# Two data routes in a two-layer trunk: how a gate row is stored and fetched, and how a normalised stream is turned

## The chip, the cores and the metric

The kernel runs on one core of a Trainium2 chip. The metric is the device time of one execution in microseconds (us): the median of several runs. A core has a matrix engine (PE, which multiplies a loaded 128x128 "stationary" tile by a moving one; the load is listed apart as PEld), a vector engine (DVE), a scalar engine (ACT), GpSimd (POOL) and a sync engine (SP). SP, ACT and POOL also issue DMA transfers, which 16 DMA engines carry out; their issues are listed under SPq, ACTq and POOLq.

## The reference

Two token streams pass through the same two layers: P, a prompt of 128 tokens, and S, a sample of 256 tokens with a cached context. Each has its own conditioning vector. Cut to what matters here:

```python
mod = silu(cvec) @ ada_w[l] + ada_b[l]             # one row of 6*1024 per stream
sh1, sc1, g1, sh2, sc2, g2 = split(mod, 6)
h = rms_norm(x, norm1_g) * (1.0 + sc1) + sh1
mix = token_mixers(h, ...)                         # gating MLP, differential attention, GQA, then w_out
x = x + g1 * mix
h = rms_norm(x, norm2_g) * (1.0 + sc2) + sh2
x = x + g2 * peer_ffn(h, ...)                      # 8 heads, top 16 of 16384 experts each
```

with `rms_norm(x, g) = x * rsqrt(mean(x*x) + 1e-6) * g` and `D = 1024`. After layer 1 a last `rms_norm` gives the output. All is float32.

## The kernel before

A layer has two stages. `chain` runs adaLN, first norm, mixers, output projection, second norm and the product-key queries for both streams; `experts` then evaluates the experts. For S it goes densely over all 16384 of them in 128 chunks (a table chunk is loaded, split into a high and a low part by ACT and DVE, and multiplied on PE). For P it gathers the chosen rows through GpSimd (`ugt`, `vgt`) and combines them on DVE. These gathers start while S is still in `chain`. In the profiled run the four stages lie at 0 to some 486 us, to 1236, to some 1622 and to 2387.

A tile framework orders the instructions: the code yields pieces of work as tasks with costs, and a scheduler with a simulated timeline sets each engine's queue and inserts the semaphores. All engine calls go through a helper at line 82, so nearly all rows show L82; work is told apart by its tiles.

The change touches four functions:

- `ada_chunk` multiplies the conditioning vectors by one of twelve 512-column chunks of `ada_w` (tile `pada`), adds the bias `ab`, and has in `row` 128 partitions: four quarters of 128 columns, 32 partitions apart, with the streams P and S in the first two partitions of each quarter. Shift and scale chunks are turned into columns (`modT`). The four gate chunks of a layer (`which` 2 and 5) are stored whole, 128x128 numbers, to a DRAM tile `grow`.
- `gate_half` fetches half a gate row (512 numbers) from `grow` to all 128 partitions: a partition's 2 KB come as four pieces of 512 bytes. `wout` uses it (tile `wo`) to scale the output projection, and `finish`, in chunk 110 of `experts`, to load the gate `G` for the update of the residual behind the experts. Both issue from ACT's queue.
- `normed_T(st, n, ...)` is the first norm (n = 0) or the second (n = 1) of a stream, block by block (128 tokens). It must give the normed, scaled and shifted stream with features on partitions. It takes the sum of squares (ACT, `junk`), the root (`rstd_of`: DVE and one POOL power; with `newton`, for S's second norm, a chain of DVE instructions on tiles `rsqi` and `rsqt`), makes a 128x128 diagonal of the roots, `dr` (ACT), and multiplies each of the block's eight 128x128 pieces by it on PE into `pt`, which scales and transposes at once. DVE and ACT then take turns to apply `modT` into `hTs` or `hTp`.
- `gate_rows` is not called.

P's first norm of layer 1 is not among these: `next_norm`, at the end of `experts`, does it with a DVE scaling in place of `x2p` and transposes by `ident`. So `normed_T` does eleven blocks: P, S, S at the first norm of layer 0, S, S at that of layer 1 (tile `x2s`, which GpSimd also stores to DRAM), and three at each second norm. `x` in layer 0's first norm is a copy that `wout` later loads again. The buffer tagged `mixT` holds the mixers' outputs up to the output projection and the queries `qT` after the second norm. For S, `hh` and `hl` are the high and low part of the second norm's result, and `pq` are the query products.

Of the kernel before, what the change touches and what calls it, by code (L numbers as in the profile page):

```python
# [9 lines left out]
F32 = mybir.dt.float32  # L10
# [5 lines left out]
AF = mybir.ActivationFunctionType  # L16
ALU = mybir.AluOpType
AX = mybir.AxisListType

D = 1024  # L20
# [78 lines left out]
def trunk_kernel(ctx, tc, xin, silu_c, wts, adab, ccol, crow, finalg, rope, ohc, io2, skt,  # L99
                 sgut, lkT, lv, ut, ug, vg, y, ck_d, cv_d, ck_g, cv_g):  # L100
    nc = tc.nc
    V, A, TE, SY, GP = nc.vector, nc.scalar, nc.tensor, nc.sync, nc.gpsimd
# [6 lines left out]
    dpool = ctx.enter_context(tc.tile_pool(name="dpool", bufs=2, space=bass.MemoryType.DRAM))  # L109

    V, TE, A, GP = Follow(V), Follow(TE), Follow(A), Follow(GP)
# [3 lines left out]
    def bank(name, st=None):  # L115
        if st is not None and name + st.name in cur["tags"]:
            name += st.name
        tag, n = cur["tags"][name]
        return cur["psum"].tile([128, 512], F32, tag=tag, name=name, bufs=n)
# [8 lines left out]
    ident = cp.tile([128, 128], F32, name="ident")  # L128
# [18 lines left out]
    def rstd_of(ss, n, width, newton=False):  # L147
        r = sm.tile([128, 8], F32, name="rstd")
        r = r[:, 0:width]
        V.tensor_scalar(r, ss, 1.0 / n, EPS, op0=ALU.mult, op1=ALU.add)  # L150
        if newton:

            i, t = sm.tile([128, 8], U32, name="rsqi")[:, 0:width], sm.tile([128, 8], F32, name="rsqt")[:, 0:width]
            V.tensor_tensor(i, r.bitcast(U32), c1[:, 0:width], op=ALU.logical_shift_right)
            V.tensor_scalar(i, i, -1.0, float(0x5f3759df), op0=ALU.mult, op1=ALU.add)
            yv = i.bitcast(F32)
            for _ in range(3):
                V.tensor_tensor(t, yv, yv, op=ALU.mult)
                V.scalar_tensor_tensor(t, t, -0.5, r, op0=ALU.mult, op1=ALU.mult)
                V.scalar_tensor_tensor(yv, t, 1.5, yv, op0=ALU.add, op1=ALU.mult)  # L160
            return yv
        GP.tensor_tensor(r, r, mhalf[:, 0:width], op=ALU.pow)
        return r

    def transposes(cols, st=None):
        pt = bank("pt", st)
        for i, c in enumerate(cols):
            TE.transpose(pt[:, i * 128:(i + 1) * 128], c, ident)
        return pt
# [4 lines left out]
    def new_layer(l):  # L174
        L = Layer()
        L.l, L.have = l, set()
        L.lam_init = 0.8 - 0.6 * math.exp(-0.3 * l)
        L.modT = sp.tile([128, 4, KC, 2], F32, name="modT")
        L.cc = sp.tile([128, 20], F32, name="cc")
        A.dma_start(L.cc, ccol[l])  # L180
        L.grow = dpool.tile([2, 2, 128, 128], F32, name="grow")
        return L

    def ada_chunk(L, j, pieces):
        which, half = divmod(j, 2)
        L.have.add(j)
        ab = sm.tile([128, 128], F32, name="ab", bufs=2)
        A.dma_start(ab, adab[L.l, j])
        ps = bank("pada")
        k = 0  # L190
        for w in pieces:
            for kk in range(w.shape[1]):
                for q in range(4):
                    TE.matmul(ps[32 * q:32 * q + 32, 0:128], sT[:, k, :], w[:, kk, q * 128:(q + 1) * 128],
                              start=(k == 0), stop=(k == KC - 1), tile_position=(0, 32 * q))
                k += 1
        row = sm.tile([128, 128], F32, name="row", bufs=2)
        V.tensor_tensor(row, ps[:, 0:128], ab, op=ALU.add)
        if which in (2, 5):
            SY.dma_start(L.grow[which // 3, half], row)  # L200
            return
        pt = transposes([row])
        pv = pt[:, 0:128].rearrange("p (q r) -> p q r", r=32)[:, :, 0:2]
        m = {0: 0, 1: 1, 3: 2, 4: 3}[which]
        dst = L.modT[:, m, half * 4:(half + 1) * 4, :]
        if m % 2:
            g = L.cc[:, (m // 2) * 8 + half * 4:(m // 2) * 8 + half * 4 + 4]
            V.scalar_tensor_tensor(dst, pv, 1.0, g[:, :, None].to_broadcast([128, 4, 2]), op0=ALU.add, op1=ALU.mult)
        else:
            V.tensor_copy(dst, pv)  # L210

    def gate_half(L, which, half, row, gb):
        src = L.grow[which, half].rearrange("(q r) c -> q r c", r=32)[:, row, :]
        A.dma_start(gb.rearrange("p (q c) -> p q c", q=4), src[None].to_broadcast([128, 4, 128]))

    def gate_rows(L, which, row, gb):
        src = L.grow[which].rearrange("h (q r) c -> h q r c", r=32)[:, :, row, :]
        A.dma_start(gb.rearrange("p (h q c) -> p h q c", h=2, q=4), src[None].to_broadcast([128, 2, 4, 128]))


    class Retrieval:
# [64 lines left out]
    def chain(L, early_ada, Ln, R0):  # L286
        l = L.l
        with ExitStack() as es:
            tp = es.enter_context(tc.tile_pool(name=f"tp{l}", bufs=1, reuse_waits=RW))
# [9 lines left out]
            def s512(st, name, w=512):  # L299
                t = tp.tile([128, 512], F32, tag="s512" + st.name, name=name, bufs=S5[0] if st is P else S5[1])  # L300
                return t[:, 0:w]
# [73 lines left out]
            def need(*js):  # L375
                while not L.have.issuperset(js):
                    yield 1.0

            def normed_T(st, n, hT, blocks):
                yield from need(*range(6 * n, 6 * n + 4))  # L380
                for b in blocks:
                    xn = st.xs[b]
                    ss = sm.tile([128, 1], F32, name="ss")
                    A.activation(s512(st, "junk").bitcast(BF16), xn, AF.Square, accum_out=ss)
                    r = rstd_of(ss, D, 1, newton=NEWT[0] and st.past and n == 1 or NEWT[2])

                    dr = s512(st, "dr", 128)
                    A.activation(dr, ident, AF.Copy, scale=r)
                    for g in range(2):
                        pt = bank("pt", st)  # L390
                        for q in range(4):
                            k = g * 4 + q
                            TE.matmul(pt[:, q * 128:(q + 1) * 128], xn[:, k * 128:(k + 1) * 128], dr, start=True, stop=True)
                        for q in range(4):
                            k = g * 4 + q
                            o = hT[:, k, b * 128:(b + 1) * 128]
                            i = pt[:, q * 128:(q + 1) * 128]
                            sca = L.modT[:, 2 * n + 1, k, st.row:st.row + 1]
                            shi = L.modT[:, 2 * n, k, st.row:st.row + 1]
                            if q % 2:  # L400
                                A.activation(o, i, AF.Identity, bias=shi, scale=sca)
                            else:
                                V.tensor_scalar(o, i, sca, shi, op0=ALU.mult, op1=ALU.add)
                    yield CN
# [427 lines left out]
            def head(st):  # L832
                if not st.past and R0 is not None and LEFT:
                    while R0.n < NSLOT + R0.LAG:
                        yield 1.0
                    for half in range(2):
                        hs = slice(half * 512, (half + 1) * 512)
                        gb = s512(st, "gb")
                        gate_half(R0.L, 1, half, st.row, gb)
                        V.tensor_tensor(gb, R0.acc[:, hs], gb, op=ALU.mult)  # L840
                        V.tensor_tensor(st.xs[0][:, hs], st.xs[0][:, hs], gb, op=ALU.add)
                    xd = dpool.tile([128, D], F32, name="x2p")
                    SY.dma_start(xd, st.xs[0])
                    st.x[0] = xd
                elif st.next:
                    st.xs, st.next = st.next, {}
                else:
                    st.xs = {}
                    for b in range(st.nb):
                        load_x(st, b)  # L850
                if not st.past:
                    alloc_mix(st)
                    if st.hT is not None:
                        return
                hp = pp if st.past else tp
                st.hT = hp.tile([128, KC, st.T], F32, name=f"hT{st.name}")
                yield from normed_T(st, 0, st.hT, range(st.nb))
# [139 lines left out]
    def experts(L, R, Ln):  # L997
        l = L.l
        last = l == DEPTH - 1
        with ExitStack() as es:  # L1000
# [246 lines left out]
            dense_loop()  # L1247

    L, R = new_layer(0), None
    for l in range(DEPTH):  # L1250
        Ln = new_layer(l + 1) if l + 1 < DEPTH else None
        R = chain(L, l == 0, Ln, R)
        R.L = L
        experts(L, R, Ln)
        L = Ln
# [86 lines left out]
```

## Time and profile before

| | us |
|---|---|
| median of three runs | 2394.32 |
| lowest, highest | 2392.46, 2396.28 |
| profiled execution, own time | 2388.71 |
| its span, first to last instruction | 2386.9 |
| mean granted PE clock | 0.968 of full |

The profiled execution is 5.6 us (0.23%) under the median; 1.8 us of its time lie outside its span. In the profile a row "out<-in" names the tile written and the tiles read, "xN" is the count, and "[2.19 <-ACT dr]" says that the engine had been idle for 2.19 us until ACT's work on `dr` released it. PEclk is the share of full clock that was granted to PE.

### The profile page before, as it was taken

The numbers are of one execution on the slowest core, as the hardware profiler recorded it, in microseconds if no ns is written. First come the engines' busy times: TensorE is split into PE (matmuls) and PEld (weight loads), VectorE is DVE, ScalarE is ACT, GpSimd is POOL, SyncE is SP. The second block draws the span as 40 slices with busy tenths as digits, with TensorE's granted clock in tenths as the row PEclk, the third lists the DMA queues.
The fourth block names the chain that finished last, engine by engine and source line by source line (L and its number), as shares of the span: only waits on it lengthen the run. The fifth ranks groups of instructions, "written<-read, shape, count | busy, mean of one in ns | idle before, by whom it ended". The sixth has DMA issues, their size and how long they took to land.

```text
span 2386.9 us, 38803 instructions
## 1 busy us (share of the span) xinstructions
PE 2218.8 (93%) x14466; PEld 1726.2 (72%) x14466; DVE 1860.0 (78%) x3795; ACT 894.4 (37%) x1848; POOL 755.0 (32%) x558
## 2 busy tenths in 40 slices
PE   6999879889999989999999998797999999999997
PEld 4446537676898768899974464586689877889996
DVE  1234668987999959899962466899889996999996
ACT  2224311143444334444442343114344343444443
POOL 0000043103544425455400002400345443545540
PEclk9998989999999999999999999899999999999999
DMA  8665699738998869999976424942899887999994
GB/s 331 211 221 175 215 356 360 275 111 293 369 376 319 287 224 400 366 375 383 367 257 203 130 89 147 356 138 90 291 356 388 336 285 260 394 386 383 380 374 161
DMA packets 201998, 681.25 MB, mean 285 GB/s; under 512 B 22225, under 2 KB 37201, under 8 KB 201809
## 3 DMA queue, kind: packets, MB, share of 16 engines
q1 hardware_dynamic: 112448, 397.66, 45.8%
q0 software_dynamic: 74160, 270.04, 30.7%
q10 hardware_dynamic: 15200, 11.07, 1.9%
q8 instruction: 114, 1.87, 0.3%
q14 instruction: 76, 0.61, 0.1%
HBM read 671.08 MB, written 7.60 MB: 284 GB/s over the span
## 4 chain that ended last, share of the span: by engine, by line
PE 71%; DVE 15%; DMA 9%; ACT 2%; issue 2%; ACTq 0%; POOL 0%; DVEq 0%; SPq 0%; POOLq 0%
PE acc L82 27%; PE pP L82 23%; PE mm L82 10%; DMA raw<-in_vg 3%; DMA w<-in_wts 3%; PE pt L82 3%; PE sc L82 2%; PE pG L82 2%; DVE ugt L82 2%; DVE si L82 2%; DVE pacc L82 2%; DVE lo L82 2%; DMA ugt<-in_ug,ei 1%; PE pq L82 1%; PE pg L82 1%
## 5 line engine op out<-in xcount | busy, mean ns | idle before, releaser
L82 POOL DMA_INDIRECT ugt<-in_ug,ei x256 | 360.8, 1409 | 975.9 <-DVE ugt L82 811.7
L82 DVE TENSOR_TENSOR lo<-raw,hi 128x1024 fp32r<-128x1024 f32 x418 | 504.9, 1220 | 108.5 <-ACT hi L82 90.4
L82 ACT ACTIVATE hi<-raw 128x1024 fp32r<-128x1024 f32 x418 | 435.6, 1057 | 343.4 <-DMA raw<-in_vg 179.4
L82 PE MATMUL acc<-hi,whl 128*128 128x512 f32 x1680 | 479.5, 400 | 19.3 <-ACT whl L82 11.2
L82 PE MATMUL pP<-hh,lo 128*128 128x256 f32 x1664 | 465.9, 280 | 8.8 <-DVE lo L82 8.7
L82 PE MATMUL pP<-hh,hi 128*128 128x256 f32 x1664 | 469.1, 282 | 1.5 <-ACT hi L82 1.5
L82 PE MATMUL pP<-hl,hi 128*128 128x256 f32 x1664 | 463.1, 278 | 0.0
L82 POOL DMA_INDIRECT vgt<-in_vg,ei x256 | 362.5, 1416 | 167.7 <-DVE pacc L82 73.2
L82 PEld LDWEIGHTS acc<-hi,whl 128*128 128x128 f32 x1680 | 313.2, 191 | 88.4 <-ACT whl L82 11.8
L82 DVE SCALAR_TENSOR_TENSOR ugt<-ugt,h 128x1024 f32<-128x1024 f32 x256 | 311.7, 1218 | 28.6 <-DMA ugt<-in_ug,ei 26.9
L82 DVE SCALAR_TENSOR_TENSOR pacc<-vgt,gz,pacc 128x1024 f32<-128x1024 f32 x254 | 324.9, 1279 | 3.9 <-DMA vgt<-in_vg,ei 3.5
L82 PEld LDWEIGHTS pP<-hh,lo 128*128 128x128 f32 x1664 | 312.6, 188 | 19.4 <-DVE lo L82 12.1
L82 PEld LDWEIGHTS pP<-hh,hi 128*128 128x128 f32 x1664 | 314.4, 189 | 10.3 <-issue 3.3
L82 PEld LDWEIGHTS pP<-hl,hi 128*128 128x128 f32 x1664 | 312.7, 188 | 3.0 <-issue 0.5
L82 PE MATMUL acc<-lo,whl 128*128 128x512 f32 x840 | 264.4, 398 | 0.1
L82 PEld LDWEIGHTS acc<-lo,whl 128*128 128x128 f32 x840 | 155.8, 191 | 31.5 <-DVE lo L82 0.7
L82 ACT ACTIVATE W<-pP 128x512 f32<-128x512 f32 x104 | 62.1, 597 | 300.0 <-PE pP L82 249.6
L82 POOL TENSOR_TENSOR rstd<-rstd,mhalf 128x1 f32<-128x1 f32 (+3 forms) x34 | 29.1, 861 | 434.1 <-DVE rstd L82 434.1
L82 ACT ACTIVATE G<-pG 128x128 f32<-128x128 f32 x512 | 94.4, 301 | 76.5 <-PE pG L82 75.5
L82 PE MATMUL mm<-w,hTs 128*128 128x512 f32 x256 | 117.6, 610 | 1.9 <-DMA w<-in_wts 1.8
L82 DVE TENSOR_TENSOR o<-ohio,i12d 128x2048 f16<-128x2048 f16 (+1 forms) x128 | 117.9, 952 | 0.8 <-DMA ohio<-in_io 0.7
L82 PE MATMUL mm<-hTs,w 128*128 128x256 f32 x512 | 117.9, 387 | 0.0
(248 smaller groups left out, 2716.2 us busy)
## 6 DMA issues: line engine op xcount, KB each, us to landing
raw<-in_vg SPq DMA_DIRECT2D x256, 512.0 KB
w<-in_wts SPq DMA_DIRECT2D x224, 512.0 KB
raw<-in_ut SPq DMA_DIRECT2D x224, 512.0 KB
w<-in_ut SPq DMA_DIRECT2D x32, 512.0 KB
ugt<-in_ug,ei POOLq DMA_INDIRECT x256
vgt<-in_vg,ei POOLq DMA_INDIRECT x256
x<-in_xin SPq DMA_DIRECT2D x5, 512.0 KB
wo<-grow ACTq DMA_DIRECT2D x8, 256.0 KB
```

Of the source, the lines that this page charges most:

```text
L82: self.last = f(*a, **k)
```

## The change

There are three edits. A layer's `grow` now holds, for each of the two gates and each stream, one unbroken row of 1024 numbers, and each gate chunk is stored by two DMAs of 4x128 numbers, one for each stream, where it was one DMA of 128x128. `gate_half` reads 512 numbers in one piece for each partition. In `normed_T` the diagonal is gone: at the first norm DVE scales the block in place; at the second ACT writes a scaled copy `xm` into the `mixT` buffer; then PE transposes by `ident`.

```diff
-        L.grow = dpool.tile([2, 2, 128, 128], F32, name="grow")
+        L.grow = dpool.tile([2, 2, D], F32, name="grow")
...
         if which in (2, 5):
-            SY.dma_start(L.grow[which // 3, half], row)
+            for r in range(2):
+                SY.dma_start(L.grow[which // 3, r, half * 512:half * 512 + 512].rearrange("(q c) -> q c", q=4),
+                             row.rearrange("(q r) c -> q r c", r=32)[:, r, :])
             return
...
     def gate_half(L, which, half, row, gb):
-        src = L.grow[which, half].rearrange("(q r) c -> q r c", r=32)[:, row, :]
-        A.dma_start(gb.rearrange("p (q c) -> p q c", q=4), src[None].to_broadcast([128, 4, 128]))
-
-    def gate_rows(L, which, row, gb):
...
+        src = L.grow[which, row:row + 1, half * 512:half * 512 + 512]
+        A.dma_start(gb, src.to_broadcast([128, 512]))
...
-                    dr = s512(st, "dr", 128)
-                    A.activation(dr, ident, AF.Copy, scale=r)
+                    if n == 0:
+                        V.tensor_scalar(xn, xn, r, None, op0=ALU.mult)
+                    else:
+
+                        if b == 0:
+                            xm = tp.tile([128, st.nb, D], F32, name="xm", tag="mixT" + st.name)
+                        A.activation(xm[:, b], xn, AF.Copy, scale=r)
+                        xn = xm[:, b]
                     for g in range(2):
                         pt = bank("pt", st)
                         for q in range(4):
                             k = g * 4 + q
-                            TE.matmul(pt[:, q * 128:(q + 1) * 128], xn[:, k * 128:(k + 1) * 128], dr, start=True, stop=True)
+                            TE.transpose(pt[:, q * 128:(q + 1) * 128], xn[:, k * 128:(k + 1) * 128], ident)
```

Since the scheduler sets the queues, the instructions also stand differently. On ACT, at S's second norm in layer 1 (`gz` are P's expert gates, unrelated to the norm), the order before is:

```order
L82 DMA wo<-grow 128x4x128
L82 ACTIVATE gz<-gz 128x4
L82 ACTIVATE junk,ss<-x 128x1024
L82 ACTIVATE gz<-gz 128x4
L82 ACTIVATE dr<-ident,rsqi 128x128
L82 ACTIVATE junk,ss<-x 128x1024
L82 ACTIVATE hTs<-pt,modT 128x128 x4
L82 ACTIVATE dr<-ident,rsqi 128x128
L82 ACTIVATE hh<-hTs 128x8x128
L82 ACTIVATE hTs<-pt,modT 128x128 x4
```

The same place on ACT after:

```order
L82 DMA wo<-grow 128x512
L82 ACTIVATE gz<-gz 128x4
L82 ACTIVATE junk,ss<-x 128x1024 x2
L82 ACTIVATE xm<-x,rsqi 128x1024 x2
L82 ACTIVATE hTs<-pt,modT 128x128 x3
L82 ACTIVATE gz<-gz 128x4
L82 ACTIVATE hTs<-pt,modT 128x128
L82 ACTIVATE hh<-hTs 128x8x128
L82 ACTIVATE hTs<-pt,modT 128x128 x4
```

Both blocks' sums of squares and both scalings now stand ahead of the first `hTs`; before, the second block's diagonal stood behind the first block's.

On PE, at S's second norm in layer 0 (`mm` is the output projection), the order before is:

```order
L82 MATMUL mm<-w,mixTs 128x512 x8
L82 MATMUL pada<-w,sT 32x128 x29
L82 MATMUL pt<-dr,x 128x128 x15
L82 MATMUL pada<-w,sT 32x128 x4
L82 MATMUL pt<-dr,x 128x128
L82 MATMUL pada<-w,sT 32x128 x6
L82 MATMUL pq<-hTs,w 128x256 x8
```

The same place on PE after:

```order
L82 MATMUL mm<-w,mixTs 128x512
L82 MATMUL pada<-w,sT 32x128 x22
L82 MATMUL pt<-ident,xm 128x128 x8
L82 MATMUL pada<-w,sT 32x128 x8
L82 MATMUL pt<-ident,xm 128x128 x8
L82 MATMUL pq<-hTs,w 128x256 x4
```

Of adaLN's products, eight now stand between the two blocks' transposes and none between these and the first `pq`.

On DVE, at S's first norm in layer 1, where the instructions ahead are those that end the update of `x2s` and prepare the attention's constants, the order after is:

```order
L82 TENSOR_SCALAR nlam<-nlam 128x1
L82 TENSOR_SCALAR rstd<-ss 128x1
L82 TENSOR_SCALAR x2s<-x2s,rstd 128x1024
L82 TENSOR_SCALAR hTs<-pt,modT 128x128 x4
L82 TENSOR_SCALAR rstd<-ss 128x1
```

Before, the same rows stood there without the scaling of `x2s`, which is new work on DVE's queue between the root and the four `hTs`.

More of the change, by code (lines that the diff above doesn't have):

```diff
@@ L212, in gate_half @@
     def gate_half(L, which, half, row, gb):
-        src = L.grow[which, half].rearrange("(q r) c -> q r c", r=32)[:, row, :]
-        A.dma_start(gb.rearrange("p (q c) -> p q c", q=4), src[None].to_broadcast([128, 4, 128]))
-    def gate_rows(L, which, row, gb):
-        src = L.grow[which].rearrange("h (q r) c -> h q r c", r=32)[:, :, row, :]
-        A.dma_start(gb.rearrange("p (h q c) -> p h q c", h=2, q=4), src[None].to_broadcast([128, 2, 4, 128]))
+        src = L.grow[which, row:row + 1, half * 512:half * 512 + 512]
+        A.dma_start(gb, src.to_broadcast([128, 512]))
     class Retrieval:
```

## The prediction, made before the changed kernel ran

> **What bounds the kernel now.** I read the page first: its engines and the chain that ended last.
>
> ```profile
> span 2386.9 us, 38803 instructions
> PE 2218.8 (93%) x14466; PEld 1726.2 (72%) x14466; DVE 1860.0 (78%) x3795; ACT 894.4 (37%) x1848; POOL 755.0 (32%) x558
> PE 71%; DVE 15%; DMA 9%; ACT 2%; issue 2%; ACTq 0%; POOL 0%; DVEq 0%; SPq 0%; POOLq 0%
> ```
>
> PE is busy for 93% of the span and is 71% of the chain. Only 168 us of PE idleness are left (2386.9 - 2218.8), and DMA's 9% of the chain is 215 us. So a time can fall in two ways: PE gets less to do, or a gap of PE closes. I therefore looked for the transfers and norms of this change beside those gaps. The gate row's tile first:
>
> ```profile
> L200 SPq DMA_DIRECT2D grow<-row x8: 320/403/692, 116.3 to 487.2; - x8
> L82 ACTq DMA_DIRECT2D wo<-grow x8: 366/384/1355, 128.6 to 1478.9; - x8
> L82 ACTq DMA_DIRECT2D G<-grow x8: 377/575/976, 863.1 to 2094.9; - x8
> ```
>
> Eight stores on SP, eight loads in the chains (`wo`), eight for the experts' update (`G`). Next the stretches just after such loads, as windows: start and end, length, busy time of PE, PEld, DVE, ACT and POOL, then PE clock, DMA share and GB/s. The first has one gate load alone, three follow `wo` loads of layer 0, one the last of layer 1, three follow `G` loads, and the last holds the load of `cr`, a row of 2304 bytes broadcast to 128 partitions.
>
> ```profile
> 1336.00:1342.00 6.00, 3.60 (x8) 1.78 (x9) 3.87 (x21) 1.04 (x4) 2.37 (x3) 0.55 0.27 42
> 131.00:142.00 11.00, 9.18 (x86) 5.06 (x85) 4.73 (x24) 1.98 (x6) 1.23 (x2) 1.00 0.69 217
> 182.00:192.00 10.00, 6.43 (x30) 2.69 (x28) 2.77 (x4) 0.46 (x1) 0.00 (x0) 1.00 0.88 170
> 238.00:249.00 11.00, 7.28 (x72) 5.66 (x71) 4.33 (x25) 2.44 (x7) 1.01 (x1) 0.94 0.57 186
> 1480.00:1492.00 12.00, 8.80 (x21) 3.68 (x20) 6.75 (x11) 0.00 (x0) 6.04 (x6) 1.00 0.62 209
> 861.00:886.00 25.00, 17.78 (x103) 13.56 (x102) 6.73 (x8) 7.40 (x14) 1.15 (x1) 0.93 0.50 157
> 2005.00:2021.00 16.00, 12.17 (x65) 8.38 (x63) 6.20 (x7) 5.33 (x7) 1.11 (x1) 0.95 0.74 234
> 963.00:1000.00 37.00, 33.53 (x212) 29.00 (x211) 30.18 (x36) 14.43 (x18) 17.28 (x12) 1.00 1.00 371
> 1235.00:1237.00 2.00, 2.00 (x10) 1.63 (x10) 0.00 (x0) 0.55 (x1) 0.00 (x0) 1.00 0.34 112
> ```
>
> A gate load alone moves 42 GB/s, so its 256 KB take 6.2 us; `cr`'s rows move 112 GB/s, at which 256 KB take 2.3 us. While a gate load is under way, the core moves 157 to 234 GB/s at a DMA share of 0.50 to 0.88 and PE has gaps; at the second `G` pair it moves 371. The chain names what PE waits for in four of these stretches (start, length, what):
>
> ```profile
> 130.11 11.03 DMA w<-in_wts
> ...
> 187.91 7.22 DMA w<-in_wts
> ...
> 237.34 10.46 DMA w<-in_wts
> ...
> 865.04 14.79 DMA raw<-in_vg
> ```
>
> These are weights, issued ahead of or behind a gate load and landing late. I read this as the gate's 512 short packets standing in front of the weights' on the DMA engines; the load itself is hardly waited for.
>
> **The gate rows, part by part.** The new load is 128 packets of 2 KB, the same 256 KB. If it takes 2.3 us where it took 6.2, it lets the weights through (6.2 - 2.3)/6.2 = 0.63 of its delay sooner. PE's idle time in the three windows of layer 0 is 11.00 - 9.18 = 1.8, 3.6 and 3.7, together 9.1 us. Gain 0.63 x 9.1 = **-6** (bounds 0, if the gaps have another cause, and -9, if they all close). The first `G` loads have 7.2 us of idleness in layer 0 and 3.8 in layer 1: 0.63 x 11 = -7. The second pair in layer 0 has 3.5 us, with DMA full anyway, so I take -1 for the second pairs: **-8** together (0 to -17, all idle time of the three windows and 2 for the pair not shown). The last `wo` load of layer 1 has 3.2 us beside it, which the load shares with P's gathers: 0.63 x 3.2 = **-2** (0 to -3.2). The remaining four `wo` loads of layer 1 and P's run beside other work: 0; if that cover were gone, a later load could only gain.
>
> A rule speaks against this. The Trainium skill, "DMA: Bandwidth & Descriptors", Specifications, puts the least transfer for full rate at 512 bytes, which the old pieces already have; by it these terms are zero. The trace disagrees as far as it goes: 42 GB/s for a lone load of such pieces.
>
> The stores go from 8 to 16 DMAs on SP, at the 403 ns median of the first row: 8 x 0.40 = 3.2 us of SP. SP is ahead of its buffers in the loops; on the path stands only the end of layer 0's chain, where a store precedes `ohio`, whose landing starts the experts, as the chain has it:
>
> ```profile
> 481.97 4.71 DMA ohio<-in_io
> ```
>
> I take **+0.5**, one issue more ahead of it (0 to +3.2).
>
> **S's second norm.** DVE and PE around it, as windows, and then its steps on the timeline (start, length, engine):
>
> ```profile
> 340.00:380.00 40.00, 28.43 (x174) 23.36 (x175) 31.65 (x95) 10.50 (x21) 15.88 (x14) 0.79 0.94 369
> 380.00:460.00 80.00, 71.73 (x518) 58.72 (x517) 79.93 (x424) 11.55 (x21) 18.22 (x19) 0.98 0.91 336
> 1484.00:1535.00 51.00, 32.31 (x115) 23.11 (x114) 40.30 (x90) 10.03 (x22) 25.70 (x23) 0.80 0.89 334
> ```
>
> ```profile
> 347.76 3.78 PE L82 MATMUL pt<-dr,x 128*128 128x128 f32 x16 [2.19 <-ACT dr L82]
> ...
> 357.03 3.36 PE L82 MATMUL pt<-dr,x 128*128 128x128 f32 x14 [5.48 <-ACT dr L82]
> ...
> 361.68 0.70 PE L82 MATMUL pq<-hTs,w 128*128 128x256 f32 x2
> ...
> 1511.70 3.78 PE L82 MATMUL pt<-dr,x 128*128 128x128 f32 x16 [12.82 <-ACT dr L82]
> ...
> 1518.14 3.78 PE L82 MATMUL pt<-dr,x 128*128 128x128 f32 x16 [2.66 <-ACT dr L82]
> ...
> 1521.71 1.92 PE L82 MATMUL pq<-hTs,w 128*128 128x256 f32 x4
> ```
>
> From the first block's products to the first query is 361.68 - 347.76 = 13.9 us in layer 0 and 10.0 in layer 1, because the second block's Newton chain stands on DVE behind P's slots and the first block's `hTs`. In the new order both roots and both scaled copies come first. The cost is two ACT passes of 128x1024 (1.05 us by the row of `hTn` below) for two diagonals of 0.40, so +0.65 a block, and PE gets 8 records a block for 16. I work out the first query in layer 0: the first block's root is ready at 347.76 less a diagonal's 0.40, 347.3; the second's Newton chain, then free of the `hTs`, some 3 us later; its copy 1.05, transposes 1.1, last `hTs` and the crossing between engines 2: about 354.5, that is 7.2 after the first root and 7.2 sooner than now. In layer 1 the first root is ready at 1511.70 - 0.40 = 1511.3, and the same 7.2 us give 1518.5, 3.2 sooner. But DVE fills the stretch behind it: 79.93 of 80 us. What PE gains counts only as far as DVE is idle: 40 - 31.65 = 8.35 us in the first window, 10.7 in the last. I take two thirds, -4.8 and -2.2: **-7** (ends +2.6, four blocks' +0.65 with nothing won, and -10.4, all of it).
>
> **The other blocks.** The groups of all diagonal products, the transposes by `ident` at the end of layer 0, the in-place scaling and the ACT pass:
>
> ```profile
> L82 PE MATMUL pt<-dr,x 128*128 128x128 f32 x144 | 31.4, 403 | 23.2 <-ACT dr L82 23.2
> L82 PE MATMUL pt<-dr,x2s 128*128 128x128 f32 x32 | 5.7, 351 | 2.8 <-ACT dr L82 2.8
> L82 PE MATMUL pt<-ident,x2p x8: 270/272/273, 1230.7 to 1231.5; 128*128 128x128 f32 x8
> L82 DVE TENSOR_SCALAR x2p<-x2p,rsqi x1: 754/754/754, 1224.8 to 1224.8; 128x1024 f32<-128x1024 f32 x1
> L82 ACT ACTIVATE hTn<-x2p x1: 1051/1051/1051, 1218.7 to 1218.7; 128x1024 f32<-128x1024 f32 x1
> ```
>
> Eleven blocks cost PE 31.4 + 5.7 = 37.1 us, 3.4 each; eight transposes take 1230.7 to 1231.5 and 0.27 for the last: 1.1. That is -2.3 a block of PE work, with +0.65 or +0.35 (0.754 for 0.40) ahead of it. Outside S's second norm and S in layer 1 there are five blocks; two stand in the start-up, where weights are awaited. Of the other three times 1.8 = 5.4, I count half, since weights are late there as well: **-2.5** (0 to -6).
>
> **S's first norm in layer 1** gets a new wait. Scaling in place overwrites `x2s`, which GpSimd is storing:
>
> ```profile
> 1240.78 0.56 POOL L82 DMA_DIRECT2D x2s<-x2s  x1 [22.46 <-DVE x2s L82]
> ...
> 1245.80 0.40 ACT L82 ACTIVATE dr<-ident,rstd 128x128 f32<-128x128 f32 x1 [0.95 <-POOL rstd L82]
> ...
> 1246.25 2.05 PE L82 MATMUL pt<-dr,x2s 128*128 128x128 f32 x16 [2.79 <-ACT dr L82]
> ...
> 1249.86 0.33 SPq L308 DMA_DIRECT2D x<-x2s  x1
> ...
> 1252.46 0.33 SPq L308 DMA_DIRECT2D x<-x2s  x1
> ...
> 1254.98 0.40 ACT L82 ACTIVATE dr<-ident,rstd 128x128 f32<-128x128 f32 x1 [1.03 <-POOL rstd L82]
> ```
>
> The reload at 1249.86 needs the same store, so the store has landed by then. The scaling moves from 1245.80 to there: +4.05, +0.35 for DVE, and eight transposes at 1.1 for products at 2.05: +3.5. The first block's `hTs` queue behind the scaling on DVE, and S's input products on PE wait for them; P's products may stand ahead. The second block's store lands before its turn (reload at 1252.46, diagonal at 1254.98), so there the block is worth 0.35 - (3.4 - 1.1) = -2.0, about -2.3 with its slow products. Net **+1.2** (-2 to +4.4).
>
> **The sum** is -6 - 8 - 2 + 0.5 - 7 - 2.5 + 1.2 = -23.8. The profiled execution goes from 2388.7 to 2364.9. The median of the runs lies 5.6 us above that execution: 2370.5, rounded to 2370. What a measurement of this kernel can tell from no change is about 0.2%, 4.8 us.
>
> **Rivals.** *The clock.* PE's clock was 0.79 and 0.80 around S's second norms, where 16 diagonal products took 3.78 us against 2.05 at 1246.25. They run slowly after a gap, and 16 records warm the clock for what follows; if 8 transposes do not, the queries run slowly instead, and the -2.3 a block and most of S's second norm return: -7 and -2.5 go, -14.3 stays: 2380. For it: the clock rows; against: `x2p`'s transposes stayed at 272 ns among dense work. The Trainium skill, "TensorE: Matmul & The Clock Gate", Part 4, says that transposes do not count for the clock as busy PE; no row here shows it alone.
>
> *The 512-byte pieces are not the limit*, but the broadcast from one place. Then -6, -8 and -2 are zero, and -7.8 is left: 2386. For it: the wait is named for weights, not for gates; against: `cr`'s 112 GB/s, also a broadcast.
>
> *The extra stores wait* (slower). Sixteen small stores hold their completion slots on SP; if each of the eight new ones holds SP until a landing such as `ohio`'s 4.71 us, and PE waits for the weight issues queued behind, that is +38, net +14: 2408. It decides from (23.8 + 4.8)/8 = 3.6 us a store. For it: one store took 692 ns to issue; against it: the median is 403.
>
> *Nothing shows*: DMA and DVE give the gaps back a few us later, since the loops are full (DMA 1.00, DVE 79.93 of 80): within 4.8 us of 2394.
>
> **How the numbers follow.** The forecast has 0.56, the clock 0.16, the 512-byte rival 0.11, nothing 0.08, the stores 0.09. The second and third lie under 2389.5: faster 0.81 with a little lost to the edge, same 0.10, slower 0.09. The forecast's own range is 2355 to 2378; the lower end 2350 takes S's second norm and the `G` loads near their far bounds, the upper 2390 takes in the clock and the 512-byte rival and leaves out no more than 2 in 10.
>
> **What would show it.** Right: `wo<-grow` stretches at over 250 GB/s with PE idle under half; `G`'s first windows the same; the first `pq` of S about 7 and 4 us nearer to the first `pt`; 88 `pt<-ident,xm` and `x` records of some 275 ns in place of 176; PE busy lower by 25. Wrong: gaps of the same length under other names, `pq` products much longer, SP waiting at `grow<-row`, or the first `hTs` of layer 1 over 5 us later.

## The result, and the profile after

The changed kernel takes 2352.53 us in the median of four runs (2349.63 to 2357.42), the kernel before, with one run more than in the table above, 2395.03. The ratio is 0.9826, with a 95% interval of 0.9807 to 0.9845: 42 us faster. The prediction said 2370, with a range of 2350 to 2390; the sign and the range held, but the gain is 1.8 times the sum, and the time lies 2.5 us inside the lower end and below the 2355 to 2378 that the forecast gave as its own range.

The profiled execution took 2352.07 us. Its page begins like this:

```profile
span 2350.3 us, 38644 instructions
PE 2203.4 (94%) x14378; PEld 1709.7 (73%) x14378; DVE 1862.4 (79%) x3800; ACT 894.1 (38%) x1843; POOL 753.3 (32%) x558
PE 71%; DVE 15%; DMA 7%; issue 4%; ACT 1%; POOL 1%; ACTq 0%; DVEq 0%; SPq 0%; POOLq 0%
```

The span is 36.6 us shorter. PE is busy for 15.4 us less and idle for 21.2 less (146.9 where it was 168.1). DMA's share of the chain went from 9% to 7%. The gate tile's issues are now these:

```profile
L201 SPq DMA_DIRECT2D grow<-row x16: 477/500/607, 113.2 to 468.1; - x16
L82 ACTq DMA_DIRECT2D wo<-grow x8: 326/333/446, 125.8 to 1455.0; - x8
L82 ACTq DMA_DIRECT2D G<-grow x8: 358/496/630, 842.7 to 2059.3; - x8
```

Sixteen stores of 0.50 us cost SP 4.8 us more than eight of 0.40 did, and their effect is not seen in PE's waits; twice a store stood on SP behind the landing of a weight, for 4.9 us in all. The stretches behind the gate loads, as windows of the changed kernel (the first holds a lone load of layer 1, three follow `wo` loads of layer 0, two the first `G` pairs):

```profile
1307.40:1309.40 2.00, 0.00 (x0) 0.00 (x0) 0.94 (x6) 0.00 (x0) 1.38 (x2) 0.78 0.35 134
127.00:138.00 11.00, 11.00 (x91) 5.82 (x90) 5.01 (x26) 1.98 (x6) 2.38 (x3) 1.00 0.87 303
177.00:187.00 10.00, 7.92 (x60) 3.52 (x62) 3.39 (x6) 1.15 (x3) 0.56 (x1) 1.00 0.70 219
230.00:241.00 11.00, 11.00 (x119) 8.15 (x118) 8.07 (x49) 3.42 (x9) 1.01 (x1) 1.00 0.81 235
842.00:867.00 25.00, 25.00 (x149) 20.05 (x148) 17.89 (x22) 10.22 (x15) 9.26 (x6) 1.00 0.80 264
1974.00:1990.00 16.00, 16.00 (x81) 11.58 (x80) 11.62 (x14) 7.81 (x11) 3.88 (x3) 1.00 0.90 314
```

The lone load fits into 2.0 us (134 GB/s for 2 us is its 256 KB), where it took 6.2. Five windows that had gaps of 1.8, 3.6, 3.7, 7.2 and 3.8 us have none but 2.1 in one. And in the 25 us behind the first `G` pair PE does 149 matmuls, where it did 103. At the old rate of 103 in 17.8 us of busy time, the closed gap of 7.2 us makes 42 of these 46; the clock there was 0.93 and is 1.00. The prediction had counted 0.63 of the gap and nothing for the clock.

S's second norm, on the timeline:

```profile
335.50 2.19 ACT L82 ACTIVATE xm<-x,rsqi 128x1024 f32<-128x1024 f32 x2 [4.58 <-DVE rsqt L82]
...
336.70 1.97 PE L82 MATMUL pt<-ident,xm 128*128 128x128 f32 x8 [8.09 <-ACT xm L82]
...
340.06 1.97 PE L82 MATMUL pt<-ident,xm 128*128 128x128 f32 x8 [0.38 <-ACT hTs L82]
...
341.82 2.27 PE L82 MATMUL pq<-hTs,w 128*128 128x256 f32 x8
...
1484.28 1.97 PE L82 MATMUL pt<-ident,xm 128*128 128x128 f32 x8 [17.89 <-ACT xm L82]
...
1489.61 2.79 PE L82 MATMUL pq<-hTs,w 128*128 128x256 f32 x6
```

From the first transpose to the first query are 5.1 us in layer 0 (13.9 before) and 5.3 in layer 1 (10.0). But the wait moved ahead: both roots are now made before the first transpose, for which PE waits 8.1 and 17.9 us. The two copies take 2.19 us. In layer 1 the longer wait takes back what the shorter stretch gives. The end of S's output products before and after, to be read with the rows of `pt` and `pq`:

```profile
1491.74 7.13 PE L82 MATMUL mm<-w,mixTs 128*128 128x512 f32 x16 [3.20 <-DMA w<-in_wts]
```

```profile
1449.49 16.90 PE L82 MATMUL mm<-w,mixTs 128*128 128x512 f32 x39
```

From the end of the last product (1498.87 and 1466.39) to the first query are 22.8 us before and 23.2 after. What is gone in layer 1 is the gap of 3.20 us for a weight, beside the last `wo` load.

S's first norm in layer 1:

```profile
1207.80 0.56 POOL L82 DMA_DIRECT2D x2s<-x2s  x1 [22.46 <-DVE x2s L82]
...
1217.13 0.75 DVE L82 TENSOR_SCALAR x2s<-x2s,rstd 128x1024 f32<-128x1024 f32 x1 [5.08 <-DMA x2s<-x2s]
...
1217.94 1.97 PE L82 MATMUL pt<-ident,x2s 128*128 128x128 f32 x8 [7.46 <-DVE x2s L82]
...
1219.70 5.34 PE L82 MATMUL mm<-w,hTn 128*128 128x512 f32 x8
```

The wait for GpSimd's store is there under its own name, "DMA x2s<-x2s", and PE stands for 7.5 us. The eight `mm` of P behind it take 5.34 us; before they took 3.60:

```profile
1248.14 3.60 PE L82 MATMUL mm<-w,hTn 128*128 128x512 f32 x8
```

### The profile page after: what moved, and what is told of

Its sections match the earlier page's. It is cut to its first block, busy times and chain, and to the rows that moved or that the text cites. A ratio compares the mean times of both kernels' runs of the same rounds, so it can differ in the third digit from the quotient of the medians.

```text
span 2350.3 us, 38644 instructions
## 1 busy us (share of the span) xinstructions
PE 2203.4 (94%) x14378; PEld 1709.7 (73%) x14378; DVE 1862.4 (79%) x3800; ACT 894.1 (38%) x1843; POOL 753.3 (32%) x558
## 4 chain that ended last, share of the span: by engine, by line
PE 71%; DVE 15%; DMA 7%; issue 4%; ACT 1%; POOL 1%; ACTq 0%; DVEq 0%; SPq 0%; POOLq 0%
PE acc L82 28%; PE pP L82 24%; PE mm L82 10%; PE pt L82 2%; DVE o L82 2%; PE sc L82 2%; PE pq L82 2%; DMA raw<-in_vg 2%; DVE ugt L82 2%; PE pG L82 1%; DVE pacc L82 1%; DMA w<-in_wts 1%; DMA ugt<-in_ug,ei 1%; DVE lo L82 1%; DVE si L82 1%
## 5 line engine op out<-in xcount | busy, mean ns | idle before, releaser
L82 POOL TENSOR_TENSOR rstd<-rstd,mhalf 128x1 f32<-128x1 f32 (+3 forms) x34 | 29.1, 861 | 429.1 <-DVE rstd L82 429.1
```

The source lines that it names most:

```text
L82: self.last = f(*a, **k)
```

## The experiments

**The gate rows alone, and the norms alone.** Each is the kernel before with one half of the change. The first:

```diff
-        L.grow = dpool.tile([2, 2, 128, 128], F32, name="grow")
+        L.grow = dpool.tile([2, 2, D], F32, name="grow")
...
-            SY.dma_start(L.grow[which // 3, half], row)
+            for r in range(2):
+                SY.dma_start(L.grow[which // 3, r, half * 512:half * 512 + 512].rearrange("(q c) -> q c", q=4),
+                             row.rearrange("(q r) c -> q r c", r=32)[:, r, :])
```

with `gate_half` as in the change.

> The kernel before with the gate rows of the change (one unbroken row a stream, two stores a chunk, one piece of 2 KB a partition); its norms keep the diagonal. Theory A (the gate loads carry the change: the steps by which the changed kernel's matmuls move ahead of the old one's lie at gate loads, 12 us in layer 0's chain and 20 us in the experts): 30 to 34 us faster than before, about 2363. Theory B (the shares of the prediction, two thirds gates and one third norms, and the rest a matter of the schedule): about 27 faster at 2368 with the norms 14. Theory C (norms carry it): within 5 us of 2395.

Measured: 2358.55 us against 2396.25, ratio 0.9844 (0.9811 to 0.9876): 38 us faster, a little more than theory A said. The second has only the change's edit of `normed_T`:

> The kernel before with the norms of the change alone; the gate rows are stored and fetched as before. Theory A: 5 to 10 us faster, about 2387, S's second norms giving 4.8 and 3.1 and the start 2.5, and the first norm of layer 1 taking 4.4 back. Theory B: 14 faster, 2381. Theory C: 2360 or less.

Measured: 2390.98 us, ratio 0.9982 (0.9963 to 1.0000): some 5 us, in an interval that ends at no change. So the gate rows carry 38 of 42 us, and theories B and C fall. Where the gate rows' 38 us come from is seen in windows between the same matmuls of both kernels (from an input product of layer 0 to P's first query; the dense stretch with the first `G` pair of layer 0; that of layer 1). Before:

```profile
164.81:216.17 51.36, 45.98 (x257) 24.55 (x258) 18.05 (x50) 18.65 (x52) 0.56 (x1) 0.81 0.67 205
873.57:929.82 56.25, 47.62 (x290) 41.99 (x289) 47.10 (x58) 23.35 (x29) 28.45 (x19) 0.94 0.87 327
1973.85:2033.55 59.70, 55.87 (x399) 41.99 (x398) 41.77 (x52) 22.53 (x53) 21.58 (x15) 0.94 0.81 266
```

With the gate rows of the change alone:

```profile
160.25:206.21 45.96, 41.40 (x258) 21.78 (x258) 17.43 (x49) 17.90 (x51) 0.56 (x1) 0.89 0.67 226
855.78:901.40 45.62, 45.12 (x290) 40.34 (x289) 44.51 (x55) 20.88 (x26) 28.82 (x19) 1.00 0.97 372
1947.90:2002.80 54.90, 53.84 (x399) 40.15 (x398) 39.96 (x49) 21.85 (x53) 21.84 (x14) 1.00 0.84 292
```

The three stretches shrink by 20.8 us. Of that, idle time is 11.7 (5.4 + 8.6 + 3.8 before, 4.6 + 0.5 + 1.1 now). The other 9.1 us are PE's busy time for the same matmuls: the granted clock was 0.81, 0.94 and 0.94, and is 0.89, 1.00 and 1.00. So a gap cost its length here, and then again what PE lost at a lower clock behind it. Two more stretches of layer 0's chain, on either side of the first one (117.33 to 164.81 and 216.17 to 292.74 before), shrink by 3.8 and 6.8 us. With them it is 31.4 us, 18.8 of idle and 12.6 of busy time; the spans of the two profiled executions are 29.1 us apart, so no other stretch is needed. The medians are 38 apart, since the execution that was profiled of the kernel before is 7.5 us quicker than its median here.

**Pieces of 512 bytes again, close together.** The changed kernel with the same order of instructions, but a gate row's quarters 640 bytes apart:

```diff
-        L.grow = dpool.tile([2, 2, D], F32, name="grow")
+        L.grow = dpool.tile([2, 2, 2, 4, 160], F32, name="grow")
...
+        src = L.grow[which, row, half][:, 0:128]
+        A.dma_start(gb.rearrange("p (q c) -> p q c", q=4), src[None].to_broadcast([128, 4, 128]))
```

> The changed kernel, order of instructions the same, but a gate row's quarters lie 640 bytes apart in DRAM, so that a load has four pieces of 512 bytes for each partition again. If the number of pieces sets a load's time (512 against 128, some 12 ns each): the lone load of layer 1 at about 1307 takes 6 us again, not 1.75, PE's gaps at the gates come back, and the time is 2352.5 + 30 = 2383. If it was the place (pieces 16 KB apart in a 64-KB tile before): loads stay under 2.5 us and the time at 2352.

Measured: 2359.75 us, ratio to before 0.9849 (0.9816 to 0.9883). The window of the lone load in this kernel:

```profile
1310.40:1312.40 2.00, 0.00 (x0) 0.00 (x0) 0.94 (x6) 0.00 (x0) 1.38 (x2) 0.64 0.46 135
```

512 pieces of 512 bytes land within 2.0 us, like 128 of 2 KB. As the main cause, the prediction's number of short packets falls: of 42 us, 36.5 stay. The time is 7 us above the 2352 that the place alone was expected to give. For most of the gain that leaves the place.

**Where a broadcast's pieces lie.** This kernel leaves out the whole computation and makes loads alone, each waiting for the one before, three of each shape.

> Not the trunk: this kernel leaves all of its computation out and only loads, one after the other on ACT's queue, a row broadcast to 128 partitions from a large input in DRAM, three times for each shape: one piece of 2 KB a partition; four pieces of 512 bytes at pitches of 640 bytes, 1, 2, 4, 8, 16, 16.5, 20, 32 and 64 KB; eight of 256 bytes at 320; one of 512 bytes; and, not broadcast, 2 KB or four times 512 bytes of its own for each partition. Its time is not compared. Theory P (pieces some KB apart, each read 128 times, are served one place at a time, pieces close together are not): packets of the 16 KB shape take about 6 us, those of 640 bytes and the single piece 1.75; at what pitch it turns is open, and 16.5 KB tells a power of two from a distance. Theory N (the old tile was slow for another reason, having just been stored for instance): every shape of four pieces takes 1.75. Theory D (number of descriptors, which the padded rows already speak against): 512 pieces take 6 us at every pitch, 1024 pieces 12.

Its transfers (issue, count, size, and the median time from issue to landing in us; `b640b` has its four pieces at 640 bytes, `b16kp` at 16.5 KB, the other `b` names give the pitch; `one512b` is a single piece a partition, `h320b` eight of 256 bytes, and the two `own` shapes are not broadcast):

```profile
one2k<-in_wts ACTq DMA_DIRECT2D x3, 256.0 KB, 3.2
b640b<-in_wts ACTq DMA_DIRECT2D x3, 256.0 KB, 3.2
b1k<-in_wts ACTq DMA_DIRECT2D x3, 256.0 KB, 3.3
b2k<-in_wts ACTq DMA_DIRECT2D x3, 256.0 KB, 3.1
b4k<-in_wts ACTq DMA_DIRECT2D x3, 256.0 KB, 4.6
b8k<-in_wts ACTq DMA_DIRECT2D x3, 256.0 KB, 7.9
b16k<-in_wts ACTq DMA_DIRECT2D x3, 256.0 KB, 7.9
b16kp<-in_wts ACTq DMA_DIRECT2D x3, 256.0 KB, 3.1
b20k<-in_wts ACTq DMA_DIRECT2D x3, 256.0 KB, 4.7
b32k<-in_wts ACTq DMA_DIRECT2D x3, 256.0 KB, 7.4
b64k<-in_wts ACTq DMA_DIRECT2D x3, 256.0 KB, 7.3
h320b<-in_wts ACTq DMA_DIRECT2D x3, 256.0 KB, 3.9
own512b<-in_wts ACTq DMA_DIRECT2D x3, 256.0 KB, 2.8
...
one512b<-in_wts ACTq DMA_DIRECT2D x3, 64.0 KB, 2.9
```

Same bytes, same number of pieces: 3.1 to 3.3 us at pitches up to 2 KB, 4.6 at 4 KB, 7.3 to 7.9 at the four multiples of 8 KB, and 3.1 again at 16.5 KB. At 20 KB, 4 KB past a multiple of 8 KB, it is 4.7, as at 4 KB. So it is no distance but the address: the times are those of pieces that, where their addresses agree modulo 8 KB, are served one after another. One such piece costs 2.9 us; three more in the same place add 5.0, some 1.7 each, and at 4 and 20 KB, where pairs agree, 2.9 + 1.7 gives the 4.6 and 4.7. It needs the broadcast: in `own512b` the four pieces of a partition lie 64 KB apart, and it takes 2.8. Theory P holds and N and D fall. Which part of the memory works so is not shown by these runs. 1024 pieces of 256 bytes take 3.9.

The Trainium skill, "DMA: Bandwidth & Descriptors", Specifications, has full rate from 512 bytes a piece on; the rows `one2k` and `b640b` agree with it, and the prediction's sentence that the trace speaks against it was wrong. The same page, Latency and other measured facts, reports slower copies at row pitches of large powers of two, from 2 MiB on; these rows show the like for a broadcast at 8 KB.

**One line in the kernel before.** The old tile had its quarters 32 rows of 512 bytes apart, 16 KB. With rows of 132 numbers they lie at 16.5 KB, and every instruction stands as before:

```diff
-        L.grow = dpool.tile([2, 2, 128, 128], F32, name="grow")
+        L.grow = dpool.tile([2, 2, 128, 132], F32, name="grow")[:, :, :, 0:128]
```

> The kernel before with one line changed: a row of the gate tile in DRAM is 132 numbers long, 128 of them used, so that the four pieces of a gate load lie 16.5 KB apart and not 16; the order of all instructions is that of the kernel before, stores and piece sizes too. Theory P (place): the lone loads of layer 1 take 1.75 us in place of 6.2, and the kernel gets most of what the one-piece rows alone gave (2358.6): 2360 to 2366, some us behind because pieces of 512 bytes still take longer in the full loops (8.4 us against 2 at S's gates in layer 0). Rival (the stores, or the order that the schedule found for the new rows, carried it): within 8 us of 2395.

Measured: 2361.69 us against 2391.51, ratio 0.9866 (0.9836 to 0.9897). Neither one piece nor the new stores nor another order is needed: padding alone gives 30 us, that is most of what the gate rows give. In this kernel the second `wo` load of layer 1, beside other work, passes in 2 us:

```profile
1348.60:1350.60 2.00, 2.00 (x6) 0.80 (x6) 0.90 (x2) 0.38 (x1) 0.00 (x0) 1.00 0.46 131
```

The remaining 8 us to the single pieces' 38 come with large intervals and are not separated further. But the number of pieces is not free in the full loops of the experts. In the padded kernel a `G` load takes 17.7 us from issue to landing (the last number), and SP's issues of tables wait for such landings (us in all, times, longest):

```profile
G<-grow ACTq DMA_DIRECT2D x8, 256.0 KB, 17.7
SPq L1014 <- DMA G<-grow: 16.0, 4, 7.9
```

With single pieces, in the changed kernel:

```profile
G<-grow ACTq DMA_DIRECT2D x8, 256.0 KB, 5.6
SPq L1017 <- DMA G<-grow: 1.2, 1, 1.2
```

The kernel before has 15.2 us of these waits, the one with pieces 640 bytes apart 15.0. What they cost in the end is not shown.

**S's first norm without the wait.** In the changed kernel, S's scaling in layer 1 goes to scratch tiles of 512 numbers and not in place (`out` holds for this norm alone):

```diff
+                        if out:
+                            xh = s512(st, "xh")
+                            V.tensor_scalar(xh, st.xs[b][:, g * 512:(g + 1) * 512], r, None, op0=ALU.mult)
```

> The changed kernel, but S's first norm in layer 1 is scaled by DVE into two 512-wide scratch tiles a block, not in place, so nothing waits for GpSimd's store of the stream; nearly all other instructions stand as in the changed kernel. If the wait for the store costs what the matmuls lose there (from 33.0 to 28.6 us ahead): 4 to 5 us faster than the changed kernel, 2348; its transposes start at about 1213 instead of 1217.9 and P's products behind them run at 450 ns instead of 667. If the attention behind it hides that: 2352.

Measured: 2350.01 us, ratio to before 0.9816 (0.9783 to 0.9848), and once more beside the changed kernel:

> The same as the kernel with S's first norm of layer 1 scaled into scratch tiles, once more beside the changed kernel. If the 6 us that its trace shows at that place last to the end: 6 us under the changed kernel, 2346. If the first comparison's 2.5 is all: 2350.

> The changed kernel unchanged, timed on the chip of this set for comparison with the others: 2350 to 2354.

Measured: 2349.22 us (0.9820, 0.9788 to 0.9852) against the changed kernel's 2350.73 (0.9823, 0.9791 to 0.9854). Its first trace shows the place as theory has it:

```profile
1212.20 0.88 DVE L82 TENSOR_SCALAR xh<-x2s,rstd 128x512 f32<-128x512 f32 x2 [0.76 <-POOL rstd L82]
...
1212.74 1.09 PE L82 MATMUL pt<-ident,xh 128*128 128x128 f32 x8 [2.88 <-DVE xh L82]
...
1213.67 3.60 PE L82 MATMUL mm<-w,hTn 128*128 128x512 f32 x8
```

PE waits 2.9 us where it waited 7.5, the transposes take 1.09 for 1.97, and P's products 3.60 for 5.34. The 32 input products from P's first on span 26.6 us here and 32.6 in the changed kernel, 6 us more. In the medians 1.5 to 2.5 us show, inside both intervals: the wait's cost at its place is shown, its lasting to the end is not. This is the fastest kernel of the study by its medians, by less than these runs can tell.

**Plain products by the identity.** In the changed kernel, `TE.transpose` becomes `TE.matmul` by `ident`: the steps are the same, with two PE records for each piece.

```diff
-                                TE.transpose(pt[:, q * 128:(q + 1) * 128], xn[:, k * 128:(k + 1) * 128], ident)
+                                TE.matmul(pt[:, q * 128:(q + 1) * 128], xn[:, k * 128:(k + 1) * 128], ident, start=True, stop=True)
```

> The changed kernel with its transposes by the identity made plain products by the identity, two PE records for each piece in place of one, as the diagonal's had been: it tells what the halved PE work of the norms is worth apart from the order of the steps. Theory 'PE work counts': 88 more records at some 140 ns, 12 us of PE, of which about half is in the open: 4 to 6 us slower than the changed kernel, 2357. Theory 'the waits count, not the work' (the second norm waits for DVE's root chain): within 2 us of it. Theory 'transposes leave the clock cold': a clock higher around S's second norm, the queries behind it quicker, and a time under the changed kernel's.

Measured: 2360.5 us (2356.58 to 2366.13) against the changed kernel's 2350.73, 10 us slower, with a ratio to before of 0.9863 (0.9834 to 0.9892). The intervals of the two just overlap, but five of its six runs lie above all five of the changed kernel. So the halved PE work seems to count, and by more than I expected (PE is busy for 2211.0 us against 2203.2), and the third theory's time did not come; but the scheduler's order moved too, and the executions profiled beside each other differ by only 2.4 us of span, so where the 10 us lie stays open. At S's first norm in layer 1 it answers the clock's question. Windows of the changed kernel (its first profile) from its first transpose on, and then of this kernel:

```profile
1217.90:1219.90 2.00, 1.96 (x9) 1.96 (x10) 0.41 (x1) 0.30 (x1) 0.00 (x0) 0.50 1.03 420
1219.90:1223.10 3.20, 3.20 (x5) 1.15 (x4) 1.14 (x3) 2.70 (x5) 0.00 (x0) 0.50 0.56 228
1223.10:1225.10 2.00, 1.94 (x5) 0.62 (x3) 0.00 (x0) 0.02 (x1) 0.00 (x0) 0.98 0.32 47
```

```profile
1220.30:1222.30 2.00, 2.00 (x9) 2.00 (x10) 0.00 (x0) 0.00 (x0) 0.00 (x0) 0.50 1.03 418
1222.30:1223.80 1.50, 1.50 (x10) 1.50 (x9) 0.41 (x1) 0.46 (x1) 0.00 (x0) 0.54 1.02 418
1223.80:1227.40 3.60, 3.58 (x10) 1.31 (x8) 1.14 (x3) 2.55 (x4) 0.00 (x0) 1.00 0.50 180
```

After the gap the clock is 0.50 in both. With plain products it is full 3.5 us after the first of them. With transposes it stays at 0.50 through their 2.0 us and for 3.2 us more of `mm`. The 2 us of transposes brought the full clock no nearer, as the Trainium skill, "TensorE: Matmul & The Clock Gate", Part 4, states. At this place the sum is a draw: 16 products and the eight `mm` take 7.1 us, eight transposes and the `mm` 7.2.

## Why the prediction was right, and where it was not

The direction and the place were right: most of PE's gaps behind the gate loads are gone. That the time fell inside the range was in part luck: the lower end had been meant for S's second norm and the `G` loads near their far bounds, and it was reached because closed gaps were worth more than their length, with a wrong cause for the slow load. The rival of no change fell with 42 us. The terms fared as follows.

- **Gate rows, -16 and +0.5 for the stores; measured -38.** The step that was mis-sized is the worth of a closed gap. I multiplied the idle time of a few windows by 0.63; in the five stretches 18.8 of 27.5 us of idle time went, and the 12.6 us of busy time that the same matmuls had taken longer, at a lower clock, had no term at all. The terms were read from an execution 5.6 us under the median: the two profiled spans are 36.6 us apart and the medians 42.5, and these 6 us are in no trace compared here. Of the forecast signs, two of the three `wo` stretches of layer 0 stayed under 250 GB/s (219 and 235). The stores cost nothing that can be seen.
- **The cause of the slow load was wrong.** I read 42 GB/s as the price of 512 short pieces. The row had the hint: at a DMA share of 0.27 the engines were idle for most of the 6.2 us. That fits engines that wait, and not engines held by the number of packets. The rival that the 512-byte size is not the limit was right in its premise, and wrong that nothing would follow: the change moved the pieces' place as well, and that was what counted most. By itself the number of pieces shows only in the experts' loops.
- **S's second norm, -7.** In layer 0 the changed kernel's trace is 4.6 us shorter from S's first output product to its first query (277.52 to 341.82, 64.3 us, where 292.74 to 361.68 was 68.9; with the gate rows alone it is 69.2), near the term's -4.8. In layer 1 the term of -2.2 failed: from the last output product to the first query nothing was gained (23.2 against 22.8). The sign that I named, the first `pq` nearer to the first `pt`, came (by 8.8 and 4.7 us), but it did not see that PE would wait ahead of the first `pt` for both roots, 17.9 us in one piece where it had been 12.8 and 2.7. The 3.2 us that layer 1 did win there are the closed gap for a weight, the load's -2.
- **S's first norm in layer 1, +1.2 (-2 to +4.4); measured +4.4** over the 32 input products from P's first on in the profiled executions, at the edge. The wait for the store was put at 4 us, and DVE stands for 5.1 ahead of the scaling; the slow clock for P's products behind it, 1.7 us, was not in the term.
- **The norms together, -8.3; measured -5** (0 to -9) alone. Its interval reaches no change.
- **The clock as a rival.** Its mechanism is there, and the sum had no term for it: transposes did not warm the clock. A transpose of `xm` took 0.43 us in the mean, where 0.275 was forecast, and eight of them 1.97 at S's second norms, where the sum has 1.1. With the norms alone PE's busy time fell by 1.1 us (2217.7 against 2218.8), where the sign had been 25 for the whole change; for the whole change it was 15.4, with 12.2 by the gate rows alone. Against it stand the 7.8 us more of busy time with plain products. How much of the norms' gain the clock took is not separated.
- **The stores as a rival** did not come up as a cost: SP issues each in 0.50 us. The wait for a landing that it spoke of is there, but small: 4.9 us in two waits, the longest 4.0, where it had put eight of 4.71.

## What to carry to other kernels

When one row is broadcast from DRAM to all partitions in several pieces, keep the pieces' addresses apart modulo 8 KB or in one run; a little padding of the tile gave 30 of the 38 us here. In the experts' full loops one piece landed sooner than four (5.6 us against 17.7 for `G`), whatever that was worth. When a transfer is slow, look at the DMA share beside its rate: a low share at a low rate means waiting for something, and counting packets will not find it. And price a closed gap on PE with the matmuls behind it at the clock they were granted, not with its length alone.

## What the runs showed of the hardware that I had not expected

- A broadcast of four 512-byte pieces takes 7.9 us from issue to landing at pitches of 8 or 16 KB and 3.1 at 16.5 KB; while such a load is under way, other queues' loads are late as well: the waits of 11.0 and 10.5 us for weights, which the chain of the kernel before names behind two `wo` loads, are not in the chain with the gate rows alone.
- After gaps of 7.3 and 7.5 us PE's clock was 0.50. Plain products brought it back in 3.5 us; 2 us of transposes did nothing toward it.
